# Down projection: its first two activation tiles come through the weight ring, all its loads stand on SyncE's queue, and x1 and the LayerNorm 2 vectors are reloaded in six pieces

## The chip, the cores and the metric

The kernel runs on one core of a Trainium2 chip. The metric is the device time of one execution in microseconds (us). TensorE (PE in the profile) does the matrix products, and loads its stationary operand beside them (PEld); VectorE (DVE), ScalarE (ACT) and GpSimd (POOL) do the elementwise work. Loads from and stores to DRAM are issued by SyncE (SP) and by ScalarE, each in the order of its own queue, and all run on the same 16 DMA engines.

## The reference, cut to what matters

One decoder layer over x of shape (1, 512, 2048) in float32: a block of three token mixers, a LayerNorm, a gated MLP with a short convolution, a second LayerNorm.

```python
x = layer_norm(DEEPNORM_ALPHA * x + mix, ln1_g, ln1_b)                    # this is x1
x = layer_norm(DEEPNORM_ALPHA * x + conv_ffn(x, w_up, conv_w, conv_b, w_down), ln2_g, ln2_b)

def conv_ffn(x, w_up, conv_w, conv_b, w_down):
    h = x @ w_up                                    # 2048 -> 2 * 5632
    hp = jnp.pad(h, ((0, 0), (CONV_WIDTH - 1, 0), (0, 0)))
    h = conv_b + sum(hp[:, j:j + T] * conv_w[j] for j in range(CONV_WIDTH))
    a, val = jnp.split(h, 2, axis=-1)
    return (jax.nn.gelu(a) * val) @ w_down          # 5632 -> 2048: the down projection
```

## The kernel before, in words

Every large product is taken in three passes over float32 operands that are split in two: `wh`, `ah` hold the rounded high part (an ACTIVATE on ScalarE), `wl`, `al` the rest (a TENSOR_TENSOR on VectorE), and each product is high·high + low·high + high·low.

The up projection runs over 44 pairs of feature tiles (`up_pair`). Each ends with gelu and the product on GpSimd (`L1076`), and stores its result, the activations of tile j (128 features by 512 tokens), to DRAM (`actd[j]`, `L1077`, issued by ScalarE). The weights pass through a pool `ring`: three slots for raw loads (tag `raw`), and two slots each for the split halves (tags `wh` and `wl`). The pools of the up projection are closed behind it (`ux.close()`), and the down projection's pool `dx` takes their memory.

The down projection makes the 2048 output columns in two halves u of 1024. Each half holds eight PSUM banks (four tiles of 128 tokens by two of 512 columns) and runs over 44 steps f. A step loads one activation tile (`af`, 256 KB, `L1095`) and one block of `w_down` (`raw`, 512 KB, `L1108`), splits both, and issues 24 matmuls of 512 columns (`down_mm`, `L1127`). I call the weights and activations of step f w0, w1, ... and a0, a1, ... In the last 8 steps of the second half the tiles are held back, so that the four token tiles are finished one after the other. `take` adds the banks to 2**0.25 times x1, which must be back in `y_` (`yo` in the profile) by then: x1 was stored to DRAM (`resd`) by the first LayerNorm. `finish` applies the second LayerNorm with its vectors `g2b` and `b2b`.

The order on each engine is set when the program is built, by a scheduler that goes by priorities and by a model of its own; an instruction then waits only for what it needs and for what stands ahead of it in its engine's queue. The reload of x1 stands in the code in step 8, before its matmuls:

```python
            if u == 0 and f == 8:
                nc.sync.dma_start(y_, resd)                                  # L1161: 4 MB
                g2b, b2b = bcast(dx, ln2_g[0], "g2b"), bcast(dx, ln2_b[0], "b2b")   # L856: 1 MB each
```

Of the kernel before, what the change touches and what calls it, by code (L numbers as in the profile page):

```python
# [9 lines left out]
F32 = mybir.dt.float32  # L10
F32R = mybir.dt.float32r
# [8 lines left out]
P = 128  # L20
T = 512
NT = 4
D = 2048
# [6 lines left out]
HP = 2000  # L30
# [9 lines left out]
def tile_trunk(ctx: ExitStack, tc: tile.TileContext, x, rel_bias, w_in, cq_gain, ckv_gain,  # L40
# [3 lines left out]
    nc = tc.nc  # L44
    cp = ctx.enter_context(tc.tile_pool(name="cp", bufs=1))
    xp = ctx.enter_context(tc.tile_pool(name="xp", bufs=32))
    ring = ctx.enter_context(tc.tile_pool(name="ring", bufs=2))
# [5 lines left out]
    def mm_bank():  # L53
        return ps.tile([P, 512], F32, tag="mm", name="mmb", bufs=4)

    def at_bank():
        return ps.tile([P, 512], F32, tag="at", name="atb", bufs=3)
# [3 lines left out]
    def av_bank():  # L61
        return ps.tile([P, 512], F32, tag="av", name="avb", bufs=1)


    def load_raw(w2, k0, nk, c0, n):
        raw = ring.tile([P, nk, n], F32, tag="raw", name="raw", bufs=3)
        nc.sync.dma_start(raw, w2[k0 * P:(k0 + nk) * P, c0:c0 + n].rearrange("(k p) n -> p k n", p=P))
        return raw

    def split_w(wh, wl, raw):  # L70
        with tc.high_priority(HP):
            nc.scalar.activation(wh, raw, AF.Copy)  # L72
            nc.vector.tensor_sub(wl, raw, wh.bitcast(F32))  # L73

    def wunit(w2, k0, nk, c0, n):
        raw = load_raw(w2, k0, nk, c0, n)
        wh = ring.tile([P, nk, n], F32R, tag="wh", name="wh")
        wl = ring.tile([P, nk, n], F32R, tag="wl", name="wl")
        split_w(wh, wl, raw)
        return wh, wl  # L80

    def split(dst_h, dst_l, src, scale=1.0):
        nc.scalar.activation(dst_h, src, AF.Copy, scale=scale)  # L83
        if scale == 1.0:
            nc.vector.tensor_sub(dst_l, src, dst_h.bitcast(F32))  # L85
        else:
            nc.vector.scalar_tensor_tensor(dst_l, src, scale, dst_h.bitcast(F32),
                                           op0=ALU.mult, op1=ALU.subtract)
# [241 lines left out]
    for kq in range(4):  # L330
# [5 lines left out]
        for k in range(4):  # L336
# [3 lines left out]
            h = xp.tile([P, T], F32R, tag="x", name="xh")  # L340
            l = xp.tile([P, T], F32R, tag="x", name="xl")
# [454 lines left out]
    for n in (2, 1, 0):  # L796
        for c in range(4):
            h = bp.tile([P, T], F32R, name=f"oh{n}{c}")
            l = bp.tile([P, T], F32R, name=f"ol{n}{c}")
# [22 lines left out]
    for d in range(KD):  # L822
        h = xp.tile([P, T], F32R, tag="x", name="mh")
        l = xp.tile([P, T], F32R, tag="x", name="ml")
# [26 lines left out]
    resd = dr.tile([P, NT, D], F32, name="resd")  # L851
    actd = dr.tile([NF, P, T], F32, name="actd")

    def bcast(pool, v, name):
        t_ = pool.tile([P, D], F32, name=name)
        nc.sync.dma_start(t_, bass.AP(tensor=v.tensor, offset=v.offset, ap=[[0, P], [1, D]]))  # L856
        return t_
# [29 lines left out]
    for c in range(4):  # L887
# [4 lines left out]
        for k0 in range(0, KD if c < 3 else KD // 2, 2):  # L892
            wh, wl = wunit(w_out[0], k0, 2, c0, n)
# [11 lines left out]
        for k0 in range(KD // 2, KD, 2):  # L905
            raw = load_raw(w_out[0], k0, 2, c0, n)
            for k in range(2):
                wh = xp.tile([P, 512], F32R, tag="x", name="lwh")
                wl = xp.tile([P, 512], F32R, tag="x", name="lwl")
# [177 lines left out]

    NL = 8
    wd = w_down[0]
    dx = ctx.enter_context(tc.tile_pool(name="dx", bufs=1, reuse_waits="tile"))  # L1090
    y_ = dx.tile([P, NT, D], F32, name="yo")

    def act_hl(f, held):
        raw = dx.tile([P, T], F32, tag="af", name="af", bufs=4)
        nc.scalar.dma_start(raw, actd[f])  # L1095
        if held:
            h = xq1.tile([P, T], F32R, tag="x", name="ah")
            l = xq1.tile([P, T], F32R, tag="x", name="al")
        else:
            h = dx.tile([P, T], F32R, tag="ah", name="ah", bufs=3)  # L1100
            l = dx.tile([P, T], F32R, tag="al", name="al", bufs=3)
        with tc.high_priority(HP):
            split(h, l, raw)
        return h, l

    def w_hl(f, u, held):
        raw = ring.tile([P, 1024], F32, tag="raw", name="raw", bufs=3)
        nc.sync.dma_start(raw, wd[f * P:(f + 1) * P, 1024 * u:1024 * u + 1024])  # L1108
        ws = []
        if held:  # L1110
            for c in range(2):
                wh = xp.tile([P, 512], F32R, tag="x", name="dwh")
                wl = xp.tile([P, 512], F32R, tag="x", name="dwl")
                split_w(wh, wl, raw[:, 512 * c:512 * c + 512])
                ws.append((wh, wl))
        else:
            wh = ring.tile([P, 1024], F32R, tag="wh", name="wh")
            wl = ring.tile([P, 1024], F32R, tag="wl", name="wl")
            split_w(wh, wl, raw)
            ws = [(wh[:, 512 * c:512 * c + 512], wl[:, 512 * c:512 * c + 512]) for c in range(2)]  # L1120
        return ws

    def down_mm(banks, t, a, w, f):
        ts_ = slice(t * P, (t + 1) * P)
        for n, (x_, m_) in enumerate(((0, 0), (0, 1), (1, 0))):
            for c in range(2):
                nc.tensor.matmul(banks[t][c], a[x_][:, ts_], w[c][m_],  # L1127
                                 start=f == 0 and n == 0, stop=f == NF - 1 and n == 2)

    def take(t, u, banks):  # L1130
        for c in range(2):
            cs_ = slice(1024 * u + 512 * c, 1024 * u + 512 * c + 512)
            nc.vector.scalar_tensor_tensor(y_[:, t, cs_], y_[:, t, cs_], ALPHA, banks[t][c], op0=ALU.mult, op1=ALU.add)
        for c in range(2):
            cs_ = slice(1024 * u + 512 * c, 1024 * u + 512 * c + 512)
            nc.vector.bn_stats(stats[:, t, 2 * u + c], y_[:, t, cs_])

    def finish(t):
        mu, r_ = layer_norm_stats(t, 4)
        for c in (3, 0, 1, 2):  # L1140
            cs_ = slice(c * 512, (c + 1) * 512)
            y = y_[:, t, cs_]
            if c == 3:
                nm = lp.tile([P, 1], F32, tag="nm", name="nm", bufs=4)
                nc.vector.tensor_scalar(nm, mu, -1.0, None, op0=ALU.mult)  # L1145
                nc.gpsimd.tensor_mul(nm, nm, r_)
                nc.scalar.activation(y, y, AF.Identity, scale=r_, bias=nm)
                nc.gpsimd.tensor_mul(y, y, g2b[:, cs_])
                nc.gpsimd.tensor_add(y, y, b2b[:, cs_])
            else:  # L1150
                nc.vector.scalar_tensor_tensor(y, y, mu, g2b[:, cs_], op0=ALU.subtract, op1=ALU.mult)
                nc.vector.scalar_tensor_tensor(y, y, r_, b2b[:, cs_], op0=ALU.mult, op1=ALU.add)
            nc.sync.dma_start(out[0, t * P:(t + 1) * P, cs_], y)

    for u in range(2):
        banks = [[mm_bank(), mm_bank()], [mm_bank(), mm_bank()], [at_bank(), at_bank()], [at_bank(), av_bank()]]
        last = NF if u == 0 else NF - NL
        for f in range(last):
            a, w = act_hl(f, False), w_hl(f, u, False)
            if u == 0 and f == 8:  # L1160
                nc.sync.dma_start(y_, resd)  # L1161
                g2b, b2b = bcast(dx, ln2_g[0], "g2b"), bcast(dx, ln2_b[0], "b2b")
            for t in range(NT):
                down_mm(banks, t, a, w, f)
        if u == 0:
            for t in range(NT):
                take(t, u, banks)
            continue

        held = [(act_hl(f, True), w_hl(f, u, True)) for f in range(last, NF)]  # L1170
        for t in range(NT):
            for f in range(last, NF):
                down_mm(banks, t, *held[f - last], f)
            take(t, u, banks)
            finish(t)
# [43 lines left out]
```

## Time and profile before

| | us |
|---|---|
| median of 3 runs | 2782.09 |
| lowest and highest of them | 2778.37 and 2784.37 |
| the profiled execution | 2781.81 |
| its span, first to last instruction | 2780.0 |
| TensorE busy in it | 2699.5 (97%) |
| VectorE, ScalarE, GpSimd busy | 1955.4, 1078.7, 485.8 |

TensorE is busy nearly all the time, so the profile is read for the places where it isn't, and for the clock that it was granted there. The mean granted clock of the execution is 0.988 of full speed. The up projection ends and the down projection begins between 2240 and 2290 us of the span.

### The profile page before, as it was taken

Reading aid. Unit: us, or ns where it says so; the run is one execution under the profiler, and the core shown is the slowest. Engines: PE = TensorE matmul, PEld = TensorE weight load, DVE = VectorE, ACT = ScalarE, POOL = GpSimd, SP = SyncE. Lnnn points to the kernel's source line nnn. Section 1 sums busy time; section 2 is a strip of 40 time slices with the busy share of each in tenths; the row PEclk is TensorE's granted clock in tenths of the full one; section 3 lists DMA queues with packets and bytes.
Section 4 is the critical chain, followed back from the end, with each engine's and each line's share of the span. In section 5 each row is a group of like instructions: output and inputs, shape, how many; then the busy total and the mean of one; then the engine's idle time right before and its main releaser. Section 6 shows DMA issues by size and latency. Waiting matters only on the chain.

```text
span 2780.0 us, 39138 instructions
## 1 busy us (share of the span) xinstructions
PE 2699.5 (97%) x15593; PEld 2343.4 (84%) x15597; DVE 1955.4 (70%) x2562; ACT 1078.7 (39%) x1613; POOL 485.8 (17%) x243
## 2 busy tenths in 40 slices
PE   8999999999999999999889999999999969999998
PEld 7788777777888788887889999999999968888886
DVE  6368988886456446427799999999999943334346
ACT  3253333334345422212445555555555522222231
POOL 0000111110000013100144434343444400000002
PEclk9999999999999999999899999999999989999999
DMA  7233333333323346534443444434344354444453
GB/s 203 79 96 113 119 118 117 111 85 90 95 91 112 96 144 189 177 118 158 130 128 113 117 122 115 126 115 122 114 117 116 114 187 139 140 142 139 141 158 107
DMA packets 362614, 348.37 MB, mean 125 GB/s; under 512 B 20387, under 2 KB 308016, under 8 KB 361792
## 3 DMA queue, kind: packets, MB, share of 16 engines
q1 hardware_dynamic: 329200, 288.77, 35.1%
q10 hardware_dynamic: 30928, 52.91, 5.8%
q0 software_dynamic: 2304, 4.20, 0.6%
q8 instruction: 122, 2.00, 0.3%
q14 instruction: 60, 0.49, 0.1%
HBM read 308.70 MB, written 33.97 MB: 123 GB/s over the span
## 4 chain that ended last, share of the span: by engine, by line
PE 92%; DVE 5%; DMA 1%; issue 1%; ACT 0%; DVEq 0%; POOL 0%; SPq 0%; ACTq 0%
PE mmb L1013 30%; PE mmb L93 13%; PE mmb L91 13%; PE mmb L92 13%; PE mmb L1127 9%; PE atb L1127 7%; PE avb L1127 2%; DVE wl L73 1%; PE atb L460 1%; PE mmb L710 1%; PE avb L536 1%; DMA af<-actd 1%; PE mmb L709 1%; PE mmb L711 1%; PE avb L537 1%
## 5 line engine op out<-in xcount | busy, mean ns | idle before, releaser
L73 DVE TENSOR_TENSOR wl<-raw,wh 128x1024 fp32r<-128x1024 f32 (+2 forms) x420 | 534.9, 1274 | 272.6 <-ACT wh L72 258.6
L1013 PE MATMUL mmb<-x1h,wh 128*128 128x256 f32 x2464 | 701.0, 285 | 7.8 <-DVE hf L1067 5.4
L1013 PE MATMUL mmb<-x1h,wl 128*128 128x256 f32 x2464 | 696.2, 283 | 6.1 <-DVE wl L73 6.1
L1013 PE MATMUL mmb<-x1l,wh 128*128 128x256 f32 x2464 | 697.5, 283 | 0.0
L72 ACT ACTIVATE wh<-raw 128x1024 fp32r<-128x1024 f32 (+2 forms) x420 | 436.9, 1040 | 649.0 <-PE mmb L92 327.6
L1013 PEld LDWEIGHTS mmb<-x1h,wh 128*128 128x128 f32 x2464 | 469.9, 191 | 14.2 <-ACT wh L72 8.4
L1013 PEld LDWEIGHTS mmb<-x1h,wl 128*128 128x128 f32 x2464 | 470.0, 191 | 7.1 <-DVE wl L73 7.1
L1013 PEld LDWEIGHTS mmb<-x1l,wh 128*128 128x128 f32 x2464 | 469.7, 191 | 0.0
L91 PE MATMUL mmb<-xh,wh 128*128 128x512 f32 (+1 forms) x1056 | 416.9, 396 | 1.2 <-ACT wh L72 1.2
L92 PE MATMUL mmb<-xl,wh 128*128 128x512 f32 (+1 forms) x1056 | 417.8, 396 | 0.0
L93 PE MATMUL mmb<-xh,wl 128*128 128x512 f32 (+1 forms) x1056 | 406.3, 396 | 0.7 <-DVE wl L73 0.6
L1005 POOL TENSOR_TENSOR ts<-ts,raw 128x1024 f32<-128x1024 f32 x88 | 264.2, 3003 | 534.4 <-DMA raw<-in_w_up_dram 267.2
L72 ACT ACTIVATE wh<-ts 128x1024 fp32r<-128x1024 f32 x176 | 186.8, 1061 | 263.4 <-PE mmb L1013 247.1
L85 DVE TENSOR_TENSOR al<-af,ah 128x512 fp32r<-128x512 f32 x88 | 60.8, 692 | 274.5 <-ACT ah L83 271.1
L93 PEld LDWEIGHTS mmb<-xh,wl 128*128 128x128 f32 (+1 forms) x1056 | 198.5, 188 | 54.3 <-issue 7.9
L91 PEld LDWEIGHTS mmb<-xh,wh 128*128 128x128 f32 (+1 forms) x1056 | 199.3, 189 | 49.2 <-issue 7.0
L92 PEld LDWEIGHTS mmb<-xl,wh 128*128 128x128 f32 (+1 forms) x1056 | 198.9, 188 | 48.3 <-issue 8.1
L1005 DVE TENSOR_TENSOR ts<-raw,raw 128x1024 f32<-128x1024 f32 x88 | 228.4, 2596 | 1.9 <-DMA raw<-in_w_up_dram 0.5
L1039 DVE SCALAR_TENSOR_TENSOR cv<-hf,cwc,cv 128x511 f32<-128x511 f32 (+1 forms) x176 | 225.4, 1281 | 1.5
L73 DVE TENSOR_TENSOR wl<-ts,wh 128x1024 fp32r<-128x1024 f32 x176 | 213.8, 1231 | 6.8 <-ACT wh L72 6.8
L83 ACT ACTIVATE ah<-af 128x512 fp32r<-128x512 f32 x88 | 55.7, 633 | 328.3 <-PE avb L1127 298.6
L865 POOL TENSOR_TENSOR rr<-ve,halfn 128x1 f32<-128x1 f32 x8 | 10.2, 1273 | 676.6 <-DVE nm L1145 500.4
(390 smaller groups left out, 4038.3 us busy)
## 6 DMA issues: line engine op xcount, KB each, us to landing
raw<-in_w_up_dram SPq DMA_DIRECT2D x186, 512.0 KB, 4.5
raw<-in_w_in_dram SPq DMA_DIRECT2D x120, 512.0 KB, 3.7
raw<-in_w_down_dram SPq DMA_DIRECT2D x88, 512.0 KB, 3.7
af<-actd ACTq DMA_DIRECT2D x88, 256.0 KB, 3.0
raw<-in_w_out_dram SPq DMA_DIRECT2D x32, 512.0 KB, 4.0
raw<-in_w_branch_dram SPq DMA_DIRECT2D x24, 512.0 KB, 4.7
thd<-th ACTq DMA_DIRECT2D x22, 512.0 KB, 2.7
th<-thd SPq DMA_DIRECT2D x22, 512.0 KB
```

Of the source, the lines that this page charges most:

```text
L72: nc.scalar.activation(wh, raw, AF.Copy)
L73: nc.vector.tensor_sub(wl, raw, wh.bitcast(F32))
L83: nc.scalar.activation(dst_h, src, AF.Copy, scale=scale)
L85: nc.vector.tensor_sub(dst_l, src, dst_h.bitcast(F32))
L91: nc.tensor.matmul(o, ah, bh, start=start, stop=False)
L92: nc.tensor.matmul(o, ah, bl, start=False, stop=False)
L93: nc.tensor.matmul(o, al, bh, start=False, stop=stop)
L460: nc.tensor.transpose(tb[:, (i - j) * P:(i - j + 1) * P], pt[:, o:o + P], ident)
L1005: eng.tensor_add(t_, a, b)
L1013: nc.tensor.matmul(bank, a[:, k], b, start=first and k == 0 and n == 0, stop=k == 7 and n == 2, skip_group_check=True)
L1039: nc.vector.scalar_tensor_tensor(c_[:, s_:], h_[:, :T - s_], cwc[:, j * 88 + f:j * 88 + f + 1], c_[:, s_:], op0=ALU.mult, op1=ALU.add)
L1127: nc.tensor.matmul(banks[t][c], a[x_][:, ts_], w[c][m_], start=f == 0 and n == 0, stop=f == NF - 1 and n == 2)
```

## The change

The activation tiles and their split halves get a pool of their own, `ax`, which is opened ahead of `dx`. Their loads are issued by SyncE instead of ScalarE. The tiles of steps 0 and 1 come in one load of 512 KB into a raw slot of `ring` (`act_first`), and their halves `fah` and `fal` take one of the two `wh` slots and one of the two `wl` slots. The reload of x1 becomes four loads of 1 MB, at steps 8, 14, 20 and 26 of the first half; `g2b` and `b2b` follow at steps 32 and 38. Each of these six is held behind the activations of its step: one column of the destination is first written by VectorE from `al` (`late`), and the load waits for that.

```diff
+    ax = ctx.enter_context(tc.tile_pool(name="ax", bufs=1, reuse_waits="tile"))
     dx = ctx.enter_context(tc.tile_pool(name="dx", bufs=1, reuse_waits="tile"))
...
     def act_hl(f, held):
-        raw = dx.tile([P, T], F32, tag="af", name="af", bufs=4)
-        nc.scalar.dma_start(raw, actd[f])
+        raw = ax.tile([P, T], F32, tag="af", name="af", bufs=4)
+        nc.sync.dma_start(raw, actd[f])
...
-            h = dx.tile([P, T], F32R, tag="ah", name="ah", bufs=3)
-            l = dx.tile([P, T], F32R, tag="al", name="al", bufs=3)
+            h = ax.tile([P, T], F32R, tag="ah", name="ah", bufs=3)
+            l = ax.tile([P, T], F32R, tag="al", name="al", bufs=3)
...
+    def act_first():
+
+        raw = ring.tile([P, 2, T], F32, tag="raw", name="raw", bufs=3)
+        nc.sync.dma_start(raw, actd[0:2].rearrange("f p t -> p f t"))
+        h = ring.tile([P, 2, T], F32R, tag="wh", name="fah")
+        l = ring.tile([P, 2, T], F32R, tag="wl", name="fal")
+        with tc.high_priority(HP):
+            split(h, l, raw)
+        return [(h[:, i], l[:, i]) for i in range(2)]
+
+    def late(dst, src, behind):
+
+        nc.vector.tensor_copy(dst[:, 0:1], behind[:, 0:1].bitcast(F32))
+        nc.sync.dma_start(dst, src)
...
+    g2b = dx.tile([P, D], F32, name="g2b")
+    b2b = dx.tile([P, D], F32, name="b2b")
+    LATE = {8 + 6 * t: (y_[:, t], resd[:, t]) for t in range(NT)}
+    LATE.update({32: (g2b, bc_src(ln2_g[0])), 38: (b2b, bc_src(ln2_b[0]))})
     for u in range(2):
...
+        if u == 0:
+            first = act_first()
         for f in range(last):
-            a, w = act_hl(f, False), w_hl(f, u, False)
-            if u == 0 and f == 8:
-                nc.sync.dma_start(y_, resd)
-                g2b, b2b = bcast(dx, ln2_g[0], "g2b"), bcast(dx, ln2_b[0], "b2b")
+            a = first[f] if u == 0 and f < 2 else act_hl(f, False)
+            w = w_hl(f, u, False)
+            if u == 0 and f in LATE:
+                late(*LATE[f], a[1])
```

On SyncE, where the up projection's last weights (`raw_21327`) are followed by the down projection's loads, before:

```order
L989 DMA raw_21327<-in_w_up_dram 128x8x128
L1108 DMA raw_21489<-in_w_down_dram 128x1024
L1108 DMA raw_21525<-in_w_down_dram 128x1024
L1108 DMA raw_21561<-in_w_down_dram 128x1024
L1108 DMA raw_21597<-in_w_down_dram 128x1024
L1108 DMA raw_21633<-in_w_down_dram 128x1024
L1161 DMA yo_21474<-resd_9438 128x8192
L856 DMA g2b_21784<-in_ln2_g_dram 128x2048
L856 DMA b2b_21786<-in_ln2_b_dram 128x2048
```

and now:

```order
L989 DMA raw_21327<-in_w_up_dram 128x8x128
L1110 DMA raw_21488<-actd_9439 128x2x512
L1127 DMA raw_21494<-in_w_down_dram 128x1024
L1127 DMA raw_21524<-in_w_down_dram 128x1024
L1127 DMA raw_21560<-in_w_down_dram 128x1024
L1127 DMA raw_21596<-in_w_down_dram 128x1024
L1096 DMA af_21554<-actd_9439 128x512
L1096 DMA af_21590<-actd_9439 128x512
L1096 DMA af_21626<-actd_9439 128x512
L1096 DMA af_21662<-actd_9439 128x512
```

The load of a0 and a1 takes the place of w0's, w0 to w3 move one place back, and a2 to a5 stand where the 6 MB of x1, `g2b` and `b2b` stood. The first of these six late loads now stands here, further down the same queue, among the loads of the steps:

```order
L1096 DMA af_21916<-actd_9439 128x512
L1120 DMA yo_21477<-resd_9438 128x2048
L1127 DMA raw_21850<-in_w_down_dram 128x1024
L1096 DMA af_21952<-actd_9439 128x512
```

One weight load and one activation load follow it per step, as before it; five more such pieces come at steps 14, 20, 26, 32 and 38.

On ScalarE, around the last store of the up projection (`actd_9439<-cv_21457`; `wh_21527<-raw_21525` is the high half of w1, a0 to a3 are `af_21483` to `af_21591`), before:

```order
L72 ACTIVATE wh_21527<-raw_21525 128x1024
L1037 ACTIVATE cv_21461<-hf2_21396,c_cb_9427,cwc_9419 128x512
L1075 ACTIVATE cv_21457<-cv_21457 128x512
L1077 DMA actd_9439<-cv_21457 128x512
L1095 DMA af_21483<-actd_9439 128x512
L1095 DMA af_21519<-actd_9439 128x512
L1095 DMA af_21555<-actd_9439 128x512
L1095 DMA af_21591<-actd_9439 128x512
L83 ACTIVATE ah_21485<-af_21483 128x512
```

and now (`raw_21494`, `raw_21524`, `raw_21560` and `raw_21596` are w0 to w3, `af_21554` is a2):

```order
L72 ACTIVATE wh_21496<-raw_21494 128x1024
L1037 ACTIVATE cv_21461<-hf2_21396,c_cb_9427,cwc_9419 128x512
L1075 ACTIVATE cv_21457<-cv_21457 128x512
L1077 DMA actd_9439<-cv_21457 128x512
L72 ACTIVATE wh_21526<-raw_21524 128x1024
L83 ACTIVATE ah_21556<-af_21554 128x512
L83 ACTIVATE ah_21592<-af_21590 128x512
L83 ACTIVATE ah_21628<-af_21626 128x512
L72 ACTIVATE wh_21562<-raw_21560 128x1024
L72 ACTIVATE wh_21598<-raw_21596 128x1024
```

The split of w0 stands where w1's stood, the four loads and the split of a0 are gone from behind the store, and the splits of w1, w2 and w3 stand there.

On TensorE, the first step of the down projection, before (the 24 matmuls take 13 rows, the first six of which are these):

```order
L1127 MATMUL mmb<-wh,ah 128x512 x2
L1127 MATMUL mmb<-wl,ah 128x512 x2
L1127 MATMUL mmb<-wh,ah 128x512 x2
L1127 MATMUL mmb<-wl,ah 128x512 x2
L1127 MATMUL atb<-wh,ah 128x512 x2
L1127 MATMUL atb<-wl,ah 128x512 x2
```

and now, the whole of the step:

```order
L1146 MATMUL mmb<-wh,fah 128x512 x4
L1146 MATMUL atb<-wh,fah 128x512 x3
L1146 MATMUL avb<-wh,fah 128x512
L1146 MATMUL mmb<-wl,fah 128x512 x2
L1146 MATMUL mmb<-wh,fal 128x512 x2
L1146 MATMUL mmb<-wl,fah 128x512 x2
L1146 MATMUL mmb<-wh,fal 128x512 x2
L1146 MATMUL atb<-wl,fah 128x512 x2
L1146 MATMUL atb<-wh,fal 128x512 x2
L1146 MATMUL atb<-wl,fah 128x512
L1146 MATMUL avb<-wl,fah 128x512
L1146 MATMUL atb<-wh,fal 128x512
```

All eight products of the high halves now come first, and the low halves of the weights and of the activations are wanted only behind them; one more row, the last `avb<-wh,fal`, ends the step. Step 1 has the same order.

## Rows read from the trace of the kernel before

**Rows 1.** The page: busy time; granted TensorE clock in 40 slices, in tenths
```profile
PE 2699.5 (97%) x15593; PEld 2343.4 (84%) x15597; DVE 1955.4 (70%) x2562; ACT 1078.7 (39%) x1613; POOL 485.8 (17%) x243
...
PEclk9999999999999999999899999999999989999999
```

**Rows 2.** Windows of 10 us: busy per engine, granted clock, DMA share, GB/s
```profile
2260.00:2270.00 10.00, 0.56 (x1) 0.50 (x2) 0.53 (x1) 0.63 (x1) 0.00 (x0) 0.50 0.97 405
2270.00:2280.00 10.00, 10.00 (x35) 7.93 (x34) 3.44 (x5) 2.96 (x4) 0.00 (x0) 0.77 0.45 142
```

**Rows 3.** The chain that ended last, 2240 to 2285: start, us, what
```profile
2253.23 15.42 DMA af<-actd
```

**Rows 4.** Timeline of TensorE: start, us, instruction [idle before, and what ended it]
```profile
2269.44 1.22 PE L1127 MATMUL mmb<-wh,ah 128*128 128x512 f32 x2 [21.69 <-ACT ah L83]
...
2277.27 0.40 PE L1127 MATMUL avb<-wh,al 128*128 128x512 f32 x1
2277.51 0.63 PE L1127 MATMUL mmb<-wh,ah 128*128 128x512 f32 x2
...
2283.12 0.63 PE L1127 MATMUL mmb<-wh,ah 128*128 128x512 f32 x2
...
2288.75 1.10 PE L1127 MATMUL mmb<-wh,ah 128*128 128x512 f32 x4
```

**Rows 5.** Timelines of ScalarE and VectorE across the boundary
```profile
2247.66 1.06 ACT L72 ACTIVATE wh<-raw 128x1024 fp32r<-128x1024 f32 x1 [1.09 <-PE mmb L1013]
...
2253.23 2.06 ACTq L1095 DMA_DIRECT2D af<-actd  x4
2268.75 0.63 ACT L83 ACTIVATE ah<-af 128x512 fp32r<-128x512 f32 x1 [18.81 <-DMA af<-actd]
...
2248.78 1.22 DVE L73 TENSOR_TENSOR wl<-raw,wh 128x1024 fp32r<-128x1024 f32 x1
```

**Rows 6.** Timeline of SyncE's queue, 2212 to 2253
```profile
2214.42 0.34 SPq L1108 DMA_DIRECT2D raw<-in_w_down_dram  x1
...
2225.62 0.34 SPq L1108 DMA_DIRECT2D raw<-in_w_down_dram  x1
...
2250.03 0.33 SPq L1108 DMA_DIRECT2D raw<-in_w_down_dram  x1
2250.47 0.36 SPq L1161 DMA_DIRECT2D yo<-resd  x1
```

**Rows 7.** DMA issues, 2250 to 2270: count, KB each, median us to landing
```profile
yo<-resd SPq DMA_DIRECT2D x1, 4096.0 KB, 14.3
...
af<-actd ACTq DMA_DIRECT2D x4, 256.0 KB, 17.4
```

**Rows 8.** One later step: SyncE, ScalarE, VectorE; landing of its weight loads, 2300 to 2500
```profile
2341.95 0.33 SPq L1108 DMA_DIRECT2D raw<-in_w_down_dram  x1
...
2345.24 1.04 ACT L72 ACTIVATE wh<-raw 128x1024 fp32r<-128x1024 f32 x1
...
2345.37 0.69 DVE L85 TENSOR_TENSOR al<-af,ah 128x512 fp32r<-128x512 f32 x1 [3.45 <-ACT ah L83]
...
DMA to landing us min/median/max: 3.5/3.7/4.7
```

**Rows 9.** Other waits of TensorE, and windows of 5 us around them
```profile
965.80 0.50 PE L91 MATMUL mmb<-xh,wh 128*128 128x512 f32 x1 [1.23 <-ACT wh L72]
...
1367.93 0.58 PE L1013 MATMUL mmb<-x1h,wl 128*128 128x256 f32 x1 [3.23 <-DVE wl L73]
...
1404.76 0.36 PE L1013 MATMUL mmb<-x1h,wh 128*128 128x256 f32 x1 [1.36 <-DVE hf L1067]
...
965.00:970.00 5.00, 3.59 (x14) 2.66 (x15) 3.69 (x5) 1.70 (x2) 0.00 (x0) 1.00 0.32 84
...
1365.00:1370.00 5.00, 2.07 (x9) 2.07 (x10) 4.10 (x2) 1.06 (x1) 1.79 (x1) 0.67 0.89 243
...
1405.00:1410.00 5.00, 5.00 (x44) 5.00 (x44) 4.99 (x6) 2.58 (x3) 2.65 (x1) 1.00 0.58 166
```

More of the change, by code (lines that the diff above doesn't have):

```diff
@@ L1104, in act_hl, with bc_src @@
         return h, l
+    def act_first():
[9 more added lines that the diff above has]
+        nc.sync.dma_start(dst, src)
+    def bc_src(v):
+        return bass.AP(tensor=v.tensor, offset=v.offset, ap=[[0, P], [1, D]])
     def w_hl(f, u, held):
```

## The prediction

> **What bounds the kernel now.** I read the page first: TensorE is busy 97% of the span, and only two of the 40 slices of granted clock show an 8, so TensorE bounds the kernel nearly everywhere [rows 1]. One of the two is the 33rd slice, 2224 to 2293.5 (a slice is 69.5 us), where the up projection passes into the down projection. What is to be won are stretches in which TensorE does nothing. The windows of 10 us show the largest: from 2260 to 2270 TensorE is busy for 0.56 us at a granted clock of 0.50, the 1.2 GHz level, while the DMA engines are 97% busy at 405 GB/s; in the next window it is busy throughout, but its clock averages 0.77 [rows 2]. The chain of waits says on what it waited: the load of an activation tile, 15.42 us from 2253.23 [rows 3]. The timeline of TensorE gives the size: it sat idle for 21.69 us before the down projection's first matmul at 2269.44, and that step, begun at the lower clock, took until 2277.51, 8.07 us, where the next two took 5.61 and 5.63 [rows 4]. I take 5.62 for a step of 24 matmuls, 0.234 for one.
>
> So the boundary costs 21.69 idle and 8.07 - 5.62 = 2.45 of slow matmuls, 24.14 us. Two things make it. The load of a0 isn't issued before 2253.23 (it stands on ScalarE's queue behind the last store of the up projection), and the tile isn't there to be split before 2268.75 [rows 5]. At 2250.47 SyncE had issued the 4 MB of x1, with 2 MB of vectors behind it [rows 6]; the four activation loads took 17.4 us to land in that company, the 4 MB 14.3 [rows 7]. The weights were not late: w0 was loaded from 2214.42, w1 from 2225.62, and w1's high half was split at 2247.66, as soon as TensorE had done with the slot [rows 5, 6].
>
> **The first step, after.** The order on SyncE puts the load of a0 and a1 where w0's was, 2214.42, and w0's where w1's was, 2225.62 [rows 6]. Their landing (3.7 us for 512 KB, at most 4.7 [rows 8]) is hidden behind the up projection, by more than 17 us. The split into `fah` and `fal` takes the place of w0's, with the same shape and so the same duration. But the two `wh` slots now have to hold `fah` too: w0's split moves to the place of w1's, 2247.66, the moment at which the up projection's last slot comes free. It takes 1.06, and TensorE follows a split by 0.06 (2268.75 + 0.63 to 2269.44 [rows 4, 5]): step 0 begins at 2248.78. The low half of w0 is ready 1.22 after 2248.78, at 2250.00 [rows 5]; the eight products that the order now puts first last 8 x 0.234 = 1.87, so this costs nothing. Without that cover TensorE would wait up to 1.22.
>
> **Steps 1 and 2: two new waits.** `fah` is read until step 1, so w1 can only take the slot of w0, after the last matmul of step 0. That begins 0.24 before the step's end and lasts 0.40 [rows 4], so it ends 0.16 behind it: 2248.78 + 5.62 + 0.16 = 2254.56. Then come 0.06, the split of 1.06 and 0.06: step 1 begins at 2255.74, where without a wait it would be 2254.40, 1.34 lost. On ScalarE this split stands behind the last store, which was issued before 2253.23 [rows 5], in time by 1.3; queued behind it are the splits of a2, a3, a4, not wanted before step 2. The low half of w1 is covered like that of w0. w2 takes the slot of `fah`, whose last reader is the third matmul from the end of step 1, 2 x 0.234 earlier: 2255.74 + 5.62 + 0.16 - 0.47 = 2261.05, and with 0.06 + 1.06 + 0.06 step 2 begins at 2262.23, 0.87 lost. w3 takes the slot of w1 right behind and is split during step 2. From step 3 on two slots serve one step's weights each, as before. Step 3 begins at 2262.23 + 5.62 = 2267.85. Before it began at 2288.75 [rows 4]. The difference, **20.90 us**, is the sum; the 24.14 that were lost become 1.03 + 1.34 + 0.87 = 3.24.
>
> a2 to a5 stand behind w3's load, issued at 2250.03 [rows 6]; four issues of some 0.35 later they are on their way together with 0.5 MB of w3 and the 0.25 MB store, 1.75 MB in all. At 405 GB/s [rows 2] that is 4.5 us, and even with 4.7 for the landing behind it a2 is there by 2260, and is split before step 2.
>
> **What moves into the steps.** The six late loads are 1 MB each. The 4 MB of x1 took 14.3, so I price one at 3.6 us, and bound it by 2.6 below (1 MB at 405 GB/s) [rows 2, 7]. They stand ahead of a weight load on SyncE. A weight load issued at 2341.95 fills the third slot; the other two are split at 2345.24 and a step later, so it is read at 2345.24 + 2 x 5.62 = 2356.48, 14.5 us after its issue. It lands in 4.7 at most [rows 8]; with 3.6 for the late load and 0.9 for an activation tile, 9.2. So it is hidden, by 5 us. If that cover were gone, six loads would cost up to 21.6.
>
> The six copies of one column on VectorE are not in the trace. Bounds: nothing, and the 0.69 of a split of 512 columns; VectorE sits idle for 3.45 us in every step [rows 8], so I take nothing (without that cover, 6 x 0.69 = 4.1). A late load waits for its copy, and the next weight load waits behind it: no longer than until the split of that step's activations, which is 0.69 long and comes early in the step.
>
> Moving the other 86 activation loads from ScalarE's queue to SyncE's adds 86 issues of some 0.33 to a queue that issues once per step of 5.62: two per step, 0.7 us. Nothing waits for ScalarE's queue there but the splits, which have room. I take nothing. The wait that a load on SyncE now adds (for `al` to free its slot) ends in the same step.
>
> **Sum.** The profiled execution took 2781.81, of which 2780.0 is its span. 2781.81 - 20.90 = 2760.91; against the median of the runs, 0.28 higher, the same sum gives 2761.2. I say **2760.9**. A difference of 0.2% (5.6 us) is about what a measurement of this kernel can tell from no change.
>
> **Rivals.**
>
> *The clock falls in the new short waits.* After a wait of 3.23 us TensorE's clock averaged 0.67 in its window, but after 1.23 and 1.36 it stayed at 1.00, at the 2.4 GHz level [rows 9]; my longest new wait is 1.34. That is for no fall, but three waits within 14 us are closer together than most. A step that begins at the lower level loses 2.45 [rows 4]; one or two such steps give 2763.4 to 2765.8. The Trainium skill, page "TensorE: Matmul & The Clock Gate", section "A second HAM failure mode: psum-queue depth-cycling", speaks against the change here: in its words TensorE "micro-idles between MM groups frequently enough" that the clock swings between its levels, and throughput falls. By that rule the time would be 2763.4 to 2765.8, by the rows above 2760.9; the trace doesn't bear the rule out for waits of this length. The same times come out if the low halves are late after all: 1.22 in each of two or three steps.
>
> *The new waits are shorter than I make them*, since an engine can react faster than 0.06, or the slots are dealt out in another way. With none of them the gain is 24.14: 2757.7.
>
> *The late loads or the single queue get in the way.* If each of the six late loads stops the weights for all of its own time, 15.6 to 21.6 us come back: 2776.5 to 2782.5, no change. Against it stand the 5 us to spare. That the change doesn't do what it says, and a0 is still late, would end in the same place; its load is issued 34 us ahead of the first matmul (2214.42 to 2248.78).
>
> *The one queue paces every step: slower.* If an activation load that waits for its slot holds the weight load behind it beyond the 14.5 us, TensorE waits in each of the 85 steps from step 3 on. From 20.90 / 85 = 0.25 us per step on the change loses; at 0.5 it is 2760.9 + 42.5 = 2803.4. For it: the queue is served in order and both kinds of load wait on it for splits. Against it: the splits that free both kinds of slot come within a microsecond or two of each other in every step, and a load would have to take 14.5 us where it takes 3.7.
>
> **How the numbers follow.** My forecast 0.78; clock or low halves 0.10; shorter waits 0.04; late loads or late a0 0.05 (0.03 of it within 0.2% of before, 0.02 just faster); one queue paces 0.03. Faster by over 0.2%: 0.78 + 0.10 + 0.04 + 0.02 = 0.94; within 0.2% 0.03; slower 0.03. The range: from the no-wait bound, 2757.7, to the two slow steps, 2765.8, and some 2 us on either side for the spread of the runs (3 to 4 us about their median before): 2756 to 2768.
>
> **What would show it.** Right: `fah` split before the up projection ends; TensorE idle some 1 us before its first down matmul, then 1.2 to 1.4 before step 1 and 0.8 to 0.9 before step 2, each released by a `wh` split on ScalarE, and no other wait of it until the end; clock 1.00 across the boundary; step 3 some 20 us after the last up matmul. Wrong: TensorE released by a load, or by a `wl` split; a window at 0.5 to 0.7 behind the boundary; a weight landing time above 10 us near steps 8 to 38; steps longer than 5.62.

## The result, and the profile after

The changed kernel takes 2762.84 us (median of 6 runs, 2759.58 to 2764.7) where the kernel before takes 2783.89 beside it (6 runs, 2778.37 to 2784.37): a ratio of 0.9928, 95% interval 0.9918 to 0.9938, 21 us faster. The profiled execution took 2762.07, of which 2760.3 is its span.

The page of the changed kernel, to be held against [rows 1]: busy time, and granted TensorE clock in 40 slices.

```profile
PE 2699.9 (98%) x15593; PEld 2343.0 (85%) x15597; DVE 1956.8 (71%) x2567; ACT 1078.7 (39%) x1612; POOL 486.9 (18%) x243
...
PEclk9999999999999999999899999999999999999999
```

TensorE does the same work in the same busy time, and the second 8 of the clock row is gone. The windows of 10 us across the boundary, where [rows 2] had 0.56 us of matmuls at 0.50:

```profile
2240.00:2250.00 10.00, 9.17 (x77) 8.96 (x76) 5.19 (x9) 4.43 (x6) 0.00 (x0) 1.00 0.05 10
2250.00:2260.00 10.00, 8.66 (x37) 6.86 (x38) 5.78 (x8) 4.29 (x7) 1.29 (x1) 1.00 0.76 243
2260.00:2270.00 10.00, 9.31 (x41) 7.26 (x40) 2.83 (x4) 3.05 (x4) 0.00 (x0) 1.00 0.69 224
```

The clock stays at 1.00, the 2.4 GHz level, and what is missing of 10 us is three short waits. The timeline of TensorE shows them; the first line is the last matmul of the up projection, the last one the start of step 3 (compare [rows 4]):

```profile
2248.89 0.28 PE L1013 MATMUL mmb<-x1h,wl 128*128 128x256 f32 x1
...
2250.20 1.19 PE L1146 MATMUL mmb<-wh,fah 128*128 128x512 f32 x4 [1.03 <-ACT wh L72]
...
2257.07 1.19 PE L1146 MATMUL mmb<-wh,fah 128*128 128x512 f32 x4 [1.15 <-ACT wh L72]
...
2263.50 1.20 PE L1146 MATMUL mmb<-wh,ah 128*128 128x512 f32 x4 [0.69 <-ACT wh L72]
...
2269.23 1.10 PE L1146 MATMUL mmb<-wh,ah 128*128 128x512 f32 x4
```

Each is released by a `wh` split on ScalarE, none by a load. Behind them, from 2290 to 2760, TensorE waits for no other engine. ScalarE's timeline (compare [rows 5]) shows what each `wh` split waited for:

```profile
2246.23 1.06 ACT L83 ACTIVATE fah<-raw 128x1024 fp32r<-128x1024 f32 x1 [3.94 <-PE mmb L1013]
...
2249.09 1.06 ACT L72 ACTIVATE wh<-raw 128x1024 fp32r<-128x1024 f32 x1 [1.09 <-PE mmb L1013]
...
2255.97 1.06 ACT L72 ACTIVATE wh<-raw 128x1024 fp32r<-128x1024 f32 x1 [4.60 <-PE avb L1146]
2256.99 1.92 ACT L83 ACTIVATE ah<-af 128x512 fp32r<-128x512 f32 x3
2262.39 2.01 ACT L72 ACTIVATE wh<-raw 128x1024 fp32r<-128x1024 f32 x2 [3.49 <-PE avb L1146]
```

All of them waited for TensorE to give a slot of the ring free: first for the up projection, then for the last product that reads the slot (the last of step 0 for w1, the third from the end of step 1 for w2). The DMA issues from 2280 to 2500 (count, KB each, median us to landing) answer to [rows 7, 8]:

```profile
raw<-in_w_down_dram SPq DMA_DIRECT2D x39, 512.0 KB, 3.7
af<-actd SPq DMA_DIRECT2D x39, 256.0 KB, 2.6
yo<-resd SPq DMA_DIRECT2D x4, 1024.0 KB, 4.9
```

**A measure with less noise.** TensorE runs the same instructions up to the boundary in all these kernels, yet the last up matmul began anywhere from 2243.93 to 2251.55 in the profiled executions (the section at the end says where that comes from). So I count each trace from the start of that matmul: when step 0 and step 3 began, and when the span ended. Times in us; the median and the ratio are of the timed runs, each ratio against the kernel before as it ran beside them; the other columns are of one profiled execution each.

| kernel | median | ratio, 95% interval | last up matmul | step 0 | step 3 | end |
|---|---|---|---|---|---|---|
| before | 2783.89 | | 2247.47 | +21.97 | +41.28 | +532.53 |
| the change | 2762.84 | 0.9918 to 0.9938 | 2248.89 | +1.31 | +20.34 | +511.41 |
| e0, the change again | 2762.37 | 0.9906 to 0.9934 | 2249.46 | +1.31 | +20.34 | +511.44 |
| e1, spread reload alone | 2771.82 | 0.9937 to 0.9964 | 2249.92 | +10.01 | +29.32 | +520.28 |
| e2, early tiles alone | 2768.17 | 0.9927 to 0.9960 | 2250.57 | +1.31 | +25.56 | +518.43 |
| e3, without the one queue | 2762.10 | 0.9906 to 0.9931 | 2243.93 | +1.31 | +20.34 | +511.37 |
| e5, without the early tiles | 2769.34 | 0.9934 to 0.9964 | 2251.55 | +8.74 | +27.77 | +518.75 |
| e8, without the spreading | 2769.07 | 0.9927 to 0.9961 | 2251.34 | +1.31 | +20.36 | +516.36 |
| e6, the six loads together | 2762.97 | 0.9910 to 0.9939 | 2248.17 | +1.31 | +20.34 | +512.83 |
| e7, e2 with short rows | 2771.35 | 0.9934 to 0.9969 | 2250.59 | +1.31 | +25.47 | +519.41 |
| e4, halves in free tiles | 2758.53 | 0.9892 to 0.9919 | 2250.09 | +0.12 | +16.99 | +508.01 |

Two profiles of the changed kernel agree within 0.03 in the last column, so it tells apart what the medians, with 2.5 to 7 us between the runs of one kernel, can't.

### The profile page after: what moved, and what is told of

It reads as the page before. It is cut to its first block, busy times and chain, and to the rows that moved or that the text cites. A ratio compares the mean times of both kernels' runs of the same rounds, so it can differ in the third digit from the quotient of the medians.

```text
span 2760.3 us, 39201 instructions
## 1 busy us (share of the span) xinstructions
PE 2699.9 (98%) x15593; PEld 2343.0 (85%) x15597; DVE 1956.8 (71%) x2567; ACT 1078.7 (39%) x1612; POOL 486.9 (18%) x243
## 4 chain that ended last, share of the span: by engine, by line
PE 93%; DVE 5%; issue 1%; ACT 0%; DMA 0%; DVEq 0%; SPq 0%; ACTq 0%
PE mmb L1013 30%; PE mmb L93 13%; PE mmb L91 13%; PE mmb L92 13%; PE mmb L1146 9%; PE atb L1146 7%; PE avb L1146 2%; DVE wl L73 1%; PE atb L460 1%; PE mmb L710 1%; PE avb L536 1%; PE mmb L709 1%; PE mmb L711 1%; PE avb L537 1%; DVE cv L1039 0%
## 5 line engine op out<-in xcount | busy, mean ns | idle before, releaser
L1013 PEld LDWEIGHTS mmb<-x1h,wh 128*128 128x128 f32 x2464 | 469.6, 191 | 14.3 <-ACT wh L72 8.4
```

Source lines behind the costliest of these rows:

```text
L1013: nc.tensor.matmul(bank, a[:, k], b, start=first and k == 0 and n == 0, stop=k == 7 and n == 2, skip_group_check=True)
```

## The experiments

My theory: the 24 us at the boundary had two causes, a load of a0 that is issued too late, and 6 MB of reload in the way of it; the change takes both away and pays some 3 us for the shared ring. Rivals: one of its three parts (early tiles, spread reload, one queue) does it all.

**e0: the changed kernel again**, with no edit.

> The changed kernel once more, as the yardstick for the runs beside it. Both theories expect its own 2762.84 us again, within the 2.5 us that its runs were apart.

2762.37, waits of 1.03, 1.15 and 0.69 again, each at the same distance from the last up matmul.

**e1: the spread reload alone.** No early tiles, and the activation loads back on ScalarE's queue.

```diff
-        nc.sync.dma_start(raw, actd[f])
+        nc.scalar.dma_start(raw, actd[f])
...
-        if u == 0:
-            first = act_first()
...
-            a = first[f] if u == 0 and f < 2 else act_hl(f, False)
+            a = act_hl(f, False)
```

> Only the spread reload: the first tiles come like all others, on ScalarE's queue behind the last store. Theory A (two causes, a late issue and a slow landing, each with its own cure): a0 is issued some 5.8 us after the last up matmul, lands in about 3 instead of 15.4, so TensorE waits about 9.5 us, step 0 runs at the lower clock and loses 2.45 again, and the later waits of the ring are gone: about 9 us slower than the changed kernel, 2771 to 2773. Theory B (the 6 MB were the whole cause): 2763 or less. Theory C (the early tiles are the whole cure): 2783, as before.

2771.82. TensorE's first down matmul, then the windows of 5 us around it, and the chain ahead of it:

```profile
2259.93 1.22 PE L1146 MATMUL mmb<-wh,ah 128*128 128x512 f32 x2 [9.73 <-ACT ah L83]
```

```profile
2255.00:2260.00 5.00, 0.07 (x1) 0.07 (x1) 0.09 (x1) 0.75 (x2) 0.30 (x1) 0.50 0.77 254
2260.00:2265.00 5.00, 5.00 (x12) 3.94 (x13) 1.89 (x3) 1.09 (x2) 0.00 (x0) 0.50 0.61 189
```

```profile
2254.04 1.27 POOL cv L1076
...
2255.33 0.33 ACTq L1077
...
2255.68 3.48 DMA af<-actd
```

Without the 6 MB beside it the load of a0 takes 3.48 us and not 15.42 [rows 3]. What is left is that it stands behind the last store: gelu and the product on GpSimd, the store's issue, the load's, the landing and the split, 10.01 us from the last up matmul. Step 0 then runs at the 1.2 GHz level: it took 8.06 us, 2.44 above 5.62. So the traffic was 41.28 - 29.32 = 11.96 us of the boundary, and the late issue with its slow step 9.89 (10.01 less the 0.12 of e4 below, which has no wait) + 2.44.

**e2: the early tiles alone.** 6 MB of reload at once at step 8, the other activation loads on ScalarE's queue.

```diff
-        nc.sync.dma_start(raw, actd[f])
+        nc.scalar.dma_start(raw, actd[f])
...
-            if u == 0 and f in LATE:
-                late(*LATE[f], a[1])
+            if u == 0 and f == 8:
+                nc.sync.dma_start(y_, resd)
+                nc.sync.dma_start(g2b, bc_src(ln2_g[0]))
+                nc.sync.dma_start(b2b, bc_src(ln2_b[0]))
```

> The early tiles a0, a1 through the ring as in the change, but the reload of x1 and the two vectors as before the change: 6 MB in one piece at step 8, and the other activation loads on ScalarE's queue. The two causes theory: step 0 begins some 1 us after the up projection, at full clock, but a2 is loaded only behind the split of w1, some 6 us after the last up matmul, into the traffic of the 6 MB, and lands some 14 to 17 us later. TensorE then waits 6 to 9 us before step 2, for a DMA, at a lower clock behind it (2.45 us for one slow step): 2769 to 2775, that is 7 to 12 us above the changed kernel. The rival, that the early tiles are the whole cure and the reload harms nothing: 2762, as the changed kernel, with the same three waits of some 1 us.

2768.17, a little below the 2769 to 2775 of the theory of two causes, and 7.0 us behind the change in the last column, the lower edge of its 7 to 12. It doesn't come from the one late landing that I expected: there are two waits. TensorE's timeline, and ScalarE's ahead of the first:

```profile
2266.65 0.72 PE L1146 MATMUL mmb<-wh,ah 128*128 128x512 f32 x2 [2.16 <-ACT ah L83]
...
2276.13 1.22 PE L1146 MATMUL mmb<-wh,ah 128*128 128x512 f32 x2 [3.59 <-ACT ah L83]
```

```profile
2264.08 2.00 ACT L72 ACTIVATE wh<-raw 128x1024 fp32r<-128x1024 f32 x2 [5.37 <-PE avb L1146]
2265.99 0.61 ACT L83 ACTIVATE ah<-af 128x512 fp32r<-128x512 f32 x1
```

In this program the split of a2 stands behind those of w2 and w3, where the change has it ahead of them. It ends at 2266.60, that of w2 at 2265.14: the order of the splits makes 2.16 us out of 0.69. (When a2 landed the trace doesn't tell; ScalarE didn't wait for it there.) The chain ahead of the second wait:

```profile
2258.56 16.43 DMA g2b<-in_ln_g_dram
...
2275.07 0.33 ACTq L1096
...
2275.44 0.64 ACT ah L83
```

ScalarE stood at the issue of a6's load until the vector `g2b` had landed, and the split of a3 stood behind that issue. In the built program a DMA's end is counted on one of a few semaphores which both queues share, and an issue can have to wait for a transfer that was counted there before. The two instructions as they stand on ScalarE, a6's load and a3's split:

```
L1096 DMA af_21698<-actd_9439 128x512 [waits DMAHW7_49,DVE_49]
L83 ACTIVATE ah_21592<-af_21590 128x512 [waits DMAHW0_49]
```

So an instruction can wait for more than what it needs and what stands ahead of it in its queue, which my words on the kernel before leave out. The load of a3 itself took 13.6 us from 2258.0 and had landed at 2271.6; split then, in 0.64, it would have been there for a start at 2266.65 + 5.73 = 2272.38. So the 6 MB cost their 7 us here through what stands in order on ScalarE (1.47 and 3.75 us of waiting, and 1.64 of a slow step behind), and not through the landing of a3.

**e3: two queues.** The change, with the activation loads from step 2 on back on ScalarE's queue.

```diff
-        nc.sync.dma_start(raw, actd[f])
+        nc.scalar.dma_start(raw, actd[f])
```

> The changed kernel with the activation loads of steps 2 to 43 and of the second half back on ScalarE's queue; early tiles and spread reload stay. If the single queue is worth nothing, as I priced it: 2762.8, within 2 us. If the loads of a2 to a5 gain from standing ahead of the last store's queue, step 2 or 3 waits for a2 or a3, a few us: 2765 to 2768.

2762.10, and +511.37 against +511.41 and +511.44: with the other two parts in place the one queue is worth nothing, and costs nothing.

**e5: no early tiles.** One queue and the spread reload are kept.

```diff
-        if u == 0:
-            first = act_first()
...
-            a = first[f] if u == 0 and f < 2 else act_hl(f, False)
+            a = act_hl(f, False)
```

> The change without the early tiles: all activation loads on SyncE's queue, the reload spread, but a0 and a1 loaded like the others, a0 behind the load of w4, some 3 us after the last up matmul begins. The load lands in 2.7 to 5 us and is split in 0.7. The two causes theory: TensorE waits 6 to 10 us before step 0, and runs step 0 at the lower clock (some 2.4 us more); the waits at steps 1 and 2 are gone: 2768 to 2772, 6 to 9 us above the changed kernel and not far from the kernel that only spreads the reload (2771.8). The rival, that the queue on which the activations are loaded makes the cure: within 2 us of 2762.

2769.34, as the theory of two causes gave, so the queue is no cure without the early tiles. It is worth something to late tiles: e1 differs from this kernel in the queue alone and ends 1.53 us later. TensorE waits once, 8.46 us, and starts slowly:

```profile
2260.29 1.22 PE L1146 MATMUL mmb<-wh,ah 128*128 128x512 f32 x2 [8.46 <-ACT ah L83]
```

```profile
2255.00:2260.00 5.00, 0.00 (x0) 0.00 (x0) 0.53 (x1) 0.39 (x1) 1.26 (x1) 0.50 0.97 282
2260.00:2265.00 5.00, 4.71 (x11) 3.72 (x12) 2.01 (x3) 1.49 (x3) 0.00 (x0) 0.51 0.72 240
```

Steps 1 and 2 follow at 5.62: without early tiles in the ring the two new waits are gone, which speaks for the ring's slots as their cause; e4 below shows it.

**e6: the six late loads together**, at step 8, still behind its `al`.

```diff
-            if u == 0 and f in LATE:
-                late(*LATE[f], a[1])
+            if u == 0 and f == 8:
+                for k in LATE:
+                    late(*LATE[k], a[1])
```

> The change with all six late loads issued at step 8, one after the other, and not one every six steps: some 6 MB ahead of the weights and activations of the next steps on the one queue. At 405 GB/s they take 15.5 us, at the 3.6 us each of the prediction 21.6; a weight load there has 14.5 us from its issue until it is read and lands by itself in 3.7, so TensorE waits 5 to 11 us once around step 10 and perhaps loses 2.45 to a slow step behind it: 2767 to 2776. If six loads of 1 MB together still hide, or have no part in what the reload cost before: 2762.4, with no TensorE wait but the three short ones.

2762.97, +1.42 in the last column: one wait of 1.20 us and no slow step, where I gave 5 to 11. The time to landing of the weight load that was issued behind the six, at 2290.00; TensorE's wait; and ScalarE ahead of it:

```profile
DMA to landing us min/median/max: 17.0/17.0/17.0
```

```profile
2309.23 1.20 PE L1146 MATMUL mmb<-wh,ah 128*128 128x512 f32 x4 [1.20 <-ACT wh L72]
```

```profile
2307.60 0.63 ACT L83 ACTIVATE ah<-af 128x512 fp32r<-128x512 f32 x1 [4.99 <-PE avb L1146]
2308.14 2.08 ACT L72 ACTIVATE wh<-raw 128x1024 fp32r<-128x1024 f32 x2
```

The block landed at 2307.0, but its split stands behind one of an activation, which waited for TensorE's step to end. TensorE wanted the block at 2307.87 (a step from 2302.25); split at its landing it would have come 2307.0 + 1.06 + 0.06 = 2308.1, some 0.3 late. So even 17 us of landing are nearly hidden. I had taken the prediction's 14.5 us for the room, but they end where the split runs, and it runs most of a step ahead of the matmuls: from the issue at 2290.00 the room was 2307.87 - 1.12 - 2290.00 = 16.8.

**e7: e2 with short rows.** The same 6 MB, cut by columns, so that a row has 2 KB.

```diff
-                nc.sync.dma_start(y_, resd)
+                for c in range(4):
+                    q_ = slice(c * 512, c * 512 + 512)
+                    nc.sync.dma_start(y_[:, :, q_], resd[:, :, q_])
```

(and the two vectors likewise)

> As e2_ring_only (6 MB of reload at step 8 on SyncE's queue, the activation loads on ScalarE's), but the reload is cut by columns, so that it moves rows of 2 KB where a partition's 32 KB of x1 lay in one row. In e2_ring_only, from 2260 to 2272, the two queues passed 194 and 242 packets, of 23 KB and 1.9 KB on average. Theory, that the DMA engines take a packet of each queue in turn, so that what a small load loses is the size of the other queue's packets: with packets of some 2 KB on both, the four activation loads (1 MB) and as much of the reload pass in some 5 us at 400 GB/s, each load lands in 3 to 8 us where it took 13.6 to 19.0, and the waits of 2.16 and 3.59 us go: some 2761 to 2764, with the rest behind the last up matmul 511 to 513 us instead of 518.4. The rival, that 6 MB in the way slow a load whatever their packets: landings of 13 to 19 us again and about 2768.

Half of it came true. The landings of those of the four activation loads for which the trace gives one, first in e2, then here:

```profile
DMA to landing us min/median/max: 13.6/16.3/19.0
```

```profile
DMA to landing us min/median/max: 3.0/5.6/8.2
```

The split of a2 now stands ahead of those of w2 and w3, at 2260.34, and the wait before step 2 is 0.70 again. But the kernel was not faster, 2771.35, above what either theory gave (2761 to 2764, and about 2768). The chain shows the same stop at the issue of a6's load, now for a weight block that SyncE had sent among the pieces; TensorE waited 4.95 before step 3, though the load of a3 had landed 3.0 us after its issue at 2258.0:

```profile
2260.67 14.26 DMA raw<-in_w_down_dram
...
2275.00 0.33 ACTq L1096
...
2275.38 0.64 ACT ah L83
```

**e8: the change without the spreading**, that is e2 with its activation loads on SyncE.

```diff
-            if u == 0 and f in LATE:
-                late(*LATE[f], a[1])
+            if u == 0 and f == 8:
+                nc.sync.dma_start(y_, resd)
+                nc.sync.dma_start(g2b, bc_src(ln2_g[0]))
+                nc.sync.dma_start(b2b, bc_src(ln2_b[0]))
```

> As the change, with early tiles and one queue, but the reload in one piece of 6 MB as before; so it differs from e2_ring_only only in the queue of the other activation loads. In the built program the loads of a2 to a5 then stand on SyncE's queue ahead of the 6 MB, and no load stands among the splits on ScalarE. In e2_ring_only and e7_small_rows ScalarE stood still from about 2266 to 2275.0 at the issue of a6's load, which ended with the landing of a vector and of a weight block, and the split of a3 stood behind it. Theory, that the 6 MB harm only what shares a queue with the splits or comes behind them: the waits of 2.16 and 3.59 us go, a5 and w5 are there in time or at most 2 us late: 2762 to 2765, and the end 511 to 514 us behind the last up matmul. The rival, that 6 MB in one piece cost this boundary what they cost in e2_ring_only on any queue: 2767 to 2771, the end at 517 to 520.

2769.07 (2763.43 to 2769.55), within the 2767 to 2771 of the rival; the end at +516.36 lies between the two theories (511 to 514, and 517 to 520). With no issue among the splits, steps 2 to 4 begin on time (step 3 at +20.36). The stop is only put off, to the weight block behind the 6 MB; TensorE's timeline, and the chain ahead of it:

```profile
2286.07 1.29 PE L1146 MATMUL mmb<-wh,ah 128*128 128x512 f32 x4 [2.96 <-ACT wh L72]
```

```profile
2267.21 17.67 DMA raw<-in_w_down_dram
```

That step began 3.13 us late and took 7.26, 1.64 above 5.62. So the one queue does have a use where big transfers are in flight: it is worth 518.43 - 516.36 = 2.1 us there. Spreading is worth 4.9 on top, and makes the queue indifferent.

**e4: the halves of a0 and a1 in free tiles.** `fah` and `fal` go into tiles of the pool `xq1`, which x1 no longer needs by then, and not into the ring's slots; the raw load stays in the ring.

```diff
-        h = ring.tile([P, 2, T], F32R, tag="wh", name="fah")
-        l = ring.tile([P, 2, T], F32R, tag="wl", name="fal")
+        hl_ = []
...
-            split(h, l, raw)
-        return [(h[:, i], l[:, i]) for i in range(2)]
+            for i in range(2):
+                h = xq1.tile([P, T], F32R, tag="x", name="fah")
+                l = xq1.tile([P, T], F32R, tag="x", name="fal")
+                split(h, l, raw[:, i])
+                hl_.append((h, l))
+        return hl_
```

> The halves of a0 and a1 go into free tiles of xq1 (its x1 blocks are last read some 8 us before the up projection ends), so that both slots of the ring are left to w0 and w1. If the three waits of 1.03, 1.15 and 0.69 us that the trace of the changed kernel shows before steps 0, 1 and 2 come from the ring's slots alone, they all go: TensorE passes the boundary without a wait, and the time falls by about 3 us against the changed kernel, to about 2759.8. If the waits come from something else (the reaction of an engine, the banks that step 0 takes over), they stay, and the time is 2762.8.

2758.53 (2753.76 to 2759.91, 4 runs): faster than both kernels, 3.8 us below e0 on the same chip and 3.4 in the last column. TensorE passes from one projection to the other without a wait:

```profile
2250.09 0.28 PE L1013 MATMUL mmb<-x1h,wl 128*128 128x256 f32 x1
2250.21 0.87 PE L1149 MATMUL mmb<-wh,fah 128*128 128x512 f32 x3
...
2255.83 1.10 PE L1149 MATMUL mmb<-wh,fah 128*128 128x512 f32 x4
...
2261.46 0.63 PE L1149 MATMUL mmb<-wh,ah 128*128 128x512 f32 x2
```

Step 0 begins 0.12 behind the last up matmul, and steps 1 and 2 follow at 5.62 and 5.63. This is the price of the ring's slots, taken away by itself.

## Why the prediction was right

**What bounds the kernel: right, and shown.** I put 24.14 us of idle and slow matmuls at the boundary; e4, which has none of it, ends 532.53 - 508.01 = 24.52 us earlier than before. By step 3 the runs split it into 11.96 for the 6 MB (before to e1), 8.98 for the early tiles (e1 to e3, which keeps the two queues, and to the change), and 3.35 that the change gives back to the ring (the change to e4). Neither part alone is enough: e1 gains 12.25 us in the last column, e2 14.10, both 21.12.

**The first step: right.** Predicted 1.31 behind the last up matmul, measured 1.31.

**The two new waits: right, a little oversized.** Step 0 and what follows it lost 8.18 - 1.31 - 5.62 = 1.25 (predicted 1.34), step 1 lost 6.43 - 5.62 = 0.81 (0.87). Step 2 took 5.73 and not 5.62, which the prediction has nowhere. Step 3 began at +20.34 where the prediction has 20.38, and the gain up to there is 20.94 for 20.90; that it fits so closely is in part luck, 0.15 too much in two terms against 0.11 left out in a third. The low halves cost nothing, as said: no `wl` split releases TensorE.

**What moves into the steps: right in the sum, two terms mis-sized.** From step 3 to the end before took 491.25 us and the change 491.07. So late loads, copies and 85 steps on one queue cost nothing together; the 0.18 I can't attribute. A late load landed in 4.8 to 4.9 us and not in 3.6: the prediction divided the 14.3 us of 4 MB by four, but one by itself takes longer than a quarter of them. A weight load took at most 6.6 us, within the 9.2 allowed for. The room that the prediction gave it, 14.5 us, ended at the split; up to the matmuls it was 16.8 in e6, where the load was issued 2 us later, so the cover holds with both. A copy took 0.15 us, within 0 to 0.69. One reading was wide: the 17.4 us of [rows 7] is the landing of one of the four activation loads, the only one for which the trace gives it; a0's, which counts, is the 15.42 of [rows 3]. No term of the sum rests on it.

**The sum.** 2760.91 for an execution that took 2762.07. The 1.16 are 1.42 by which the last up matmul began later, less 0.04 and 0.18 of gain beyond the sum, and 0.04 between span and time. Against the median of its runs, 2762.84, the forecast is 1.9 low; but the kernel before took 2783.89 beside it and not 2781.81, so the gain by the medians is 21.05 for 20.90.

**The rivals.** *The clock falls*: no. Three waits of 1.03, 1.15 and 0.69 within 14 us left it at 1.00. The rule of the Trainium skill that spoke against the change, page "TensorE: Matmul & The Clock Gate", section "A second HAM failure mode: psum-queue depth-cycling", is not borne out for waits of this length: the windows from 2240 to 2270 show 1.00. Three waits at one boundary are not a kernel that idles like this throughout; no run here tries that. *Shorter waits*: no, they were what the slots make them, and e4 shows the time without them. *Late loads in the way*: no; even six together cost 1.4, most of it by the order of two splits. *The queue paces every step*: no; e3 without it ends within 0.07.

## What to carry to other kernels

Where two phases meet, ask of the first tile of the second phase both when its load can be issued and what will be in flight beside it: here each cure alone gave more than half of the gain (12.25 and 14.10 of 21.12 us). A load that waits for nothing but a slot belongs ahead of the phase's end, and its halves in memory that nobody is waiting for: a slot borrowed from a ring of two delays its next users by a split each. A bulk reload with no near deadline goes in pieces between the steps, and on a queue where no split stands behind an issue.

## What the runs showed of the hardware

**Two queues share the DMA engines by packets, not by bytes.** In e2, from 2260 to 2272, both queues had work; the columns are packets, MB and share of 16 engines, q1 being SyncE's and q10 ScalarE's:

```profile
q1 hardware_dynamic: 194, 4.51, 88.1%
q10 hardware_dynamic: 242, 0.45, 10.0%
```

About as many packets passed on one as on the other (from 2261 to 2270, 112 and 110), but a packet of the reload carried 23 KB and one of the activations 1.9 KB, so that the small loads got a tenth of the engines. With packets of 2 KB on both sides (e7) two of them landed in 3.0 and 8.2 us instead of 13.6 and 19.0. The Trainium skill, page "DMA: Bandwidth & Descriptors", section "Queues, rings and completion order", says that each engine goes round its queues and drains a whole packet before it turns; the 194 and 242 packets agree with it. What the page calls a packet is several descriptors, and no run here shows how many of the trace's packets that is. The change takes the small loads out of this race by spreading the reload over the steps, not by the queue (e3).

**The clock after a wait.** TensorE's clock stayed at 1.00 after waits of 0.69 to 1.20 and after one of 2.16 (e2). After 2.96 (e8) and 3.59 (e2) a step took 1.64 more than 5.62, after 4.95 (e7) 2.66, after 8.46 and 9.73 (e5, e1) 2.16 and 2.44. The granted clock around these steps in e8, e2 and e7, in this order (those of e5 and e1 are above, 0.51 and 0.50):

```profile
2285.00:2290.00 5.00, 3.93 (x11) 3.13 (x12) 2.45 (x2) 2.08 (x2) 0.00 (x0) 0.70 0.86 306
```

```profile
2273.00:2278.00 5.00, 1.87 (x5) 1.51 (x6) 0.83 (x2) 1.26 (x2) 0.00 (x0) 0.81 1.02 393
```

```profile
2275.00:2280.00 5.00, 3.94 (x9) 3.14 (x10) 0.69 (x1) 0.63 (x1) 0.00 (x0) 0.50 1.04 377
```

**The spacing of the matmuls.** Behind a short wait the first ones of a step are further apart: in step 2 of the change the ninth starts 1.98 us behind the first, where 8 x 0.234 is 1.87, and the same 0.11 is in the step behind the 1.20 of e6, which took 5.73. In steps 0 and 1, which read `fah` and `fal`, those from the ninth on are closer. The ninth and the last of step 0, then of step 2:

```profile
2252.14 0.61 PE L1146 MATMUL mmb<-wl,fah 128*128 128x512 f32 x2
...
2255.54 0.39 PE L1146 MATMUL avb<-wh,fal 128*128 128x512 f32 x1
...
2265.48 0.63 PE L1146 MATMUL mmb<-wl,ah 128*128 128x512 f32 x2
...
2268.99 0.40 PE L1146 MATMUL avb<-wh,al 128*128 128x512 f32 x1
```

That is 3.40 us for 15 in step 0, 0.227 for one, and 0.234 in step 2. A wait alone doesn't do it, for step 2 has one too; and in e4, whose `fah` and `fal` lie outside the ring, it is 0.234 in steps 0 and 1. It is part of why step 1 began 0.09 earlier than predicted. I have no cause for it.

**Where the runs differ.** The same program reached the boundary at 2243.93 to 2251.55. From 1300 to 1500 the granted clock averaged 0.97 in the earliest of these executions (e3) and 0.92 in the latest (e5). Whole times go with the clock in the same way (e3's runs: 2757.1 at a mean clock of 0.995, 2764.41 at 0.991), which is why the last column of the table is the better measure of this change. Why the clock differs there no run shows.
